# U also laid out transposed, longer DRAM runs, six accumulators and another dealing of gathered rows in a hybrid decoder block

## The chip, the cores and the metric

One core of a Trainium2 chip. The metric is the device time of one execution in microseconds. A run's time is that of the whole program; its profiled execution gives the trace.

## What is computed

One decoder block on x of 1024 tokens x 1024 channels, float32. Two mixers run on the normed input: stick-breaking attention (8 heads of 128) and a gated delta rule (8 heads, chunks); both are projected back, weighted by sigmoid gates and summed into x through w_out. Then a PEER feed-forward follows. Each token makes 8 queries, each of two halves, and takes the best 16 of 128 keys for either half, so the best 16 of the pairs: 128 experts of 16384 per token. With them

```
u   = u_tab[expert]                       # rows of 1024
act = gelu(einsum('td,ted->te', h, u))
out = einsum('te,ted->td', gate * act, v_tab[expert])
```

The tables u and v are 16384 x 1024 each, 64 MB.

## The kernel before

The tokens go in two halves of 512 (`half`, L1061): projections with stick-breaking attention (`sb_attend`), delta rule (`gdn_head`), gate logits, `merge`, `out_proj`, `ffn_norm`, `route`. Products of float32 are made as three matmuls of split operands (`mm3`, L68): `split` (L58) copies a value to a rounded `hi` on ACT and subtracts it to `lo` on DVE.

**Weights.** `load_w` (L87) loads a block of 256 columns of a weight in two DMAs of 512 KB on SP's queue; a run in DRAM is 256 floats, 1 KB. `keys_T` (L649) transposes the keys once at the start and keeps them in DRAM.

**The feed-forward goes two ways.** Four blocks of 128 tokens (0, 1, 4, 5) fetch each expert row that they need: `gather_rows` (L993) is a generator of 1024 steps. Each step gathers 128 rows of 4 KB, one per token, with an indirect DMA on POOL (L1016) into one of four row buffers (six in the dense loop), and uses them with one DVE instruction: L1019 (dot product, first 128 steps of a block) or L1021 (weighted sum, the other 128). Below, such a step is called a row. Rows are dealt to the other work: each call of `gather(phase)` (L1045) adds PACE[phase] (L30) to what is due, and as many rows are issued with the lowest priority, each ordered on DVE behind the last DVE instruction so far. The scheduler may place them later, not earlier. Only the second half has rows: 64 calls in attention, 80 in the delta rule, 16 each in logits, merge and out, 64 in the gate table, and 128 in the dense loop.

**The other four blocks (2, 3, 6, 7; 512 tokens) are computed densely against all 16384 experts.** `gate_table` (L808) makes, block by block, a table of gate weights: for 32 tokens at a time PE multiplies one-hot matrices (L851), ACT evicts into `gt_stg` (two buffers, L852) and SP writes 2 MB to `g_d` in DRAM (L854), 16 writes in all. A run of the write is 16 KB, a run of the read (L906) 32 floats x 4, 512 bytes. The dense loop (L965 to L986) then takes 128 chunks of 128 experts:

- `prep` (L870): load 128 rows of U, 512 KB; 8 transposes on PE (L877) into the bank pair `pz0`; split each half from PSUM (ACT and DVE).
- `scores` (L882): 24 matmuls of 512 columns (L891, L893) into `pmm`, gelu on ACT (L895). It prepares the next chunk's U.
- `weigh` (L915): multiply by the gate table (L922), split (L926, L913).
- `values` (L931): load 512 KB of V in runs of 2 KB, and split.
- 24 value matmuls per chunk (L71 to L73 through `mm3`) into four accumulators, two banks `pc` and two `pz1`, evicted after 8 chunks by DVE (L974). Then the next group begins, for the other 512 columns or the next 8 chunks.

Seven chunks of scores are asked for (PRE) while the gate table is made, between the blocks; the scheduler can run two more ahead, since `pmm` has two banks.

Of the kernel before, what the change touches and what calls it, by code (L numbers as in the profile page):

```python
# [7 lines left out]
F32 = mybir.dt.float32  # L8
F32R = mybir.dt.float32r
# [9 lines left out]
P = 128  # L19
D = 1024  # L20
# [4 lines left out]
GT = 32  # L25
KD = D // P
# [3 lines left out]
PACE = dict(sb=2.2, gdn=1.5, logits=2.5, merge=2.5, out=0.5, route=0, table=0.1, dense=5.25)  # L30
# [4 lines left out]
C_GS, C_GG = 7184, 8208  # L35


class Block:
# [48 lines left out]
    def load_w(self, src, c0, n=CB):  # L87

        hi = self.wp.tile([P, KD, n], F32R, name="w_hi")
        lo = self.wp.tile([P, KD, n], F32R, name="w_lo")  # L90
        for k0 in range(0, KD, 4):
            raw = self.wraw.tile([P, 4, n], F32, name="w_raw")
            self.nc.sync.dma_start(raw, src[k0 * P:(k0 + 4) * P, c0:c0 + n].rearrange("(k p) n -> p k n", p=P))
            for k in range(k0, k0 + 4, 2):
                self.split(hi[:, k:k + 2], lo[:, k:k + 2], raw[:, k - k0:k - k0 + 2])
        return hi, lo
# [131 lines left out]
    def sb_qk(self, hx, pair, col):  # L228

        nc, pool = self.nc, self.pj  # L230
        w = self.load_w(self.i["w_in"][0], col + pair * CB)
# [30 lines left out]
    def sb_v(self, hx, pair, v):  # L262
        w = self.load_w(self.i["w_in"][0], C_V + pair * CB)
# [110 lines left out]
    def gdn_gates(self, half, hx, pool):  # L374
# [3 lines left out]
        w = self.load_w(self.i["w_in"][0], C_BA, 16)  # L378
# [35 lines left out]
    def gdn_proj(self, half, hx, pair):  # L414
# [3 lines left out]
        for n, col in enumerate((C_GQ, C_GK, C_GV, C_GZ)):  # L418
            w = self.load_w(self.i["w_in"][0], col + pair * CB)
# [158 lines left out]
    def gate_logits(self, half, hx):  # L578
        nc = self.nc
        for br, gcol in enumerate((C_GS, C_GG)):  # L580
            for c in range(D // CB):
                w = self.load_w(self.i["w_in"][0], gcol + c * CB)
# [8 lines left out]
    def merge(self, half, mg, x2, pool):  # L591
        nc = self.nc
        part = pool.tile([P, KD, TH], F32, name="part")
        for br, (osrc, wname) in enumerate(((self.o_sb, "w_branch_sb"), (self.o_gdn, "w_branch_gdn"))):
# [8 lines left out]
            for c in range(D // CB):  # L603
                wb = self.load_w(self.i[wname][0], c * CB)
# [21 lines left out]
    def out_proj(self, half, mg, x2):  # L626

        nc = self.nc
        for c in range(2):
            w = self.load_w(self.i["w_out"][0], c * CB)  # L630
# [7 lines left out]
        ws = [self.load_w(self.i["w_out"][0], c * CB) for c in (2, 3)]  # L638
# [9 lines left out]

    def keys_T(self, kp):  # L649

        nc = self.nc
        kt = kp.tile([P, H, 2, P], F32, name="kt")
        for t, nm in enumerate(("peer_keys1", "peer_keys2")):
            raw = kp.tile([P, H, P], F32, name="kraw", bufs=2)
            nc.sync.dma_start(raw, self.i[nm][0].rearrange("h n d -> n h d"))
            for h0 in range(0, H, 4):
                ps = self.pzt([P, 4, P])
                for h in range(4):
                    nc.tensor.transpose(ps[:, h], raw[:, h0 + h], self.ident)
                nc.scalar.copy(kt[:, h0:h0 + 4, t], ps)  # L660
        nc.sync.dma_start(self.keys_d, kt)
# [510 lines left out]
```

## Time and profile before

| | us |
|---|---|
| median of 3 runs | 3900.24 |
| lowest, highest | 3888.91, 3903.44 |
| profiled execution | 3908.46 |
| its span | 3906.7 |
| mean granted clock of TensorE, as a share of full speed | 0.971 |

The span runs from the first to the last instruction; 1.8 us of the execution lie around it. TensorE shows 94% of the span, DVE 79%, ACT 45%, POOL 33%. Matmuls are pipelined, so what a matmul costs is read from start to start and not from its length. The chain that ended last lies on PE for 28% of the span, and the dense loop's score matmuls are its largest part.

### The profile page before, as it was taken

To read this page: it belongs to the slowest core of one execution; us is meant where nothing else is said; L and a number is where in the kernel's file an instruction comes from. 1 tells how busy PE (TensorE), PEld (TensorE's weight loads), DVE (VectorE), ACT (ScalarE), POOL (GpSimd) and SP (SyncE) were. 2 spreads that over 40 slices of the span, in tenths; PEclk is the share of its full clock that TensorE was granted. 3 is DMA by queue.
4 is the path that set the end of the run, shared out by engine and by line. 5 is a ranking of instruction groups with operands and counts; after the bars stand their busy time and mean duration, and the time that the engine had idled before them with its cause. 6 is when DMAs were issued, how large, how long until landed. Compare 5 with 4: busy or idle time off the path is not lost. (4 is left out here: it accounts for less than half of the span.)

```text
span 3906.7 us, 55712 instructions
## 1 busy us (share of the span) xinstructions
PE 3674.3 (94%) x19976; PEld 3077.4 (79%) x19976; DVE 3089.5 (79%) x6330; ACT 1753.0 (45%) x3986; POOL 1298.8 (33%) x1034
## 2 busy tenths in 40 slices
PE   8999999999999999998877995899999999999997
PEld 7878888787777688886666884788888888888886
DVE  4345554349988988888789998899898899899898
ACT  6755555333777655543322994222222222222321
POOL 0000000000144322233341113655566555566555
PEclk9999999999999999999888998999999999999998
DMA  5221114552387766578884568899999999999998
GB/s 141 86 83 50 55 49 127 167 190 88 103 275 263 240 196 190 161 229 290 309 283 147 214 230 305 307 353 363 334 362 355 332 354 352 335 360 351 351 347 297
DMA packets 448230, 939.72 MB, mean 241 GB/s; under 512 B 44113, under 2 KB 239697, under 8 KB 445521
## 3 DMA queue, kind: packets, MB, share of 16 engines
q0 software_dynamic: 147456, 536.94, 39.1%
q1 hardware_dynamic: 300496, 399.22, 30.5%
q8 instruction: 157, 2.57, 0.3%
q14 instruction: 121, 0.98, 0.1%
HBM read 865.27 MB, written 70.25 MB: 239 GB/s over the span
## 5 line engine op out<-in xcount | busy, mean ns | idle before, releaser
L1016 POOL DMA_INDIRECT gb_row<-peer_u,expert x512 | 670.0, 1309 | 1879.1 <-DVE expert L796 1013.5
L1016 POOL DMA_INDIRECT gb_row<-peer_v,expert x512 | 627.6, 1226 | 714.9 <-DVE gb_h L1021 464.1
L1021 DVE SCALAR_TENSOR_TENSOR gb_h<-gb_row,gb_act,gb_h 128x1024 f32<-128x1024 f32 x512 | 656.1, 1281 | 60.6 <-DMA gb_row<-peer_v,expert 33.1
L1019 DVE SCALAR_TENSOR_TENSOR gb_row<-gb_row,gb_h 128x1024 f32<-128x1024 f32 x512 | 613.0, 1219 | 97.4 <-DMA gb_row<-peer_u,expert 77.6
L891 PE MATMUL mm<-hf,ut 128*128 128x512 f32 x2048 | 514.2, 398 | 0.0
L891 PEld LDWEIGHTS mm<-hf,ut 128*128 128x128 f32 x2048 | 376.1, 188 | 70.7
L63 DVE TENSOR_TENSOR w_lo<-w_raw,w_hi 128x512 fp32r<-128x512 f32 (+1 forms) x456 | 298.4, 676 | 166.7 <-ACT w_hi L62 128.5
L62 ACT CAST w_hi<-w_raw 128x512 fp32r<-128x512 f32 (+1 forms) x456 | 262.9, 615 | 275.6 <-PE mm L72 127.5
L71 PE MATMUL mm<-h,w_hi 128*128 128x512 f32 (+1 forms) x784 | 322.4, 411 | 4.0 <-ACT pj L587 4.0
L73 PE MATMUL mm<-h,w_lo 128*128 128x512 f32 (+1 forms) x784 | 319.9, 408 | 0.0
L72 PE MATMUL mm<-h,w_hi 128*128 128x512 f32 (+1 forms) x784 | 319.2, 407 | 0.0
L71 PE MATMUL mm<-w_hi,h 128*128 128x256 f32 x1024 | 301.3, 295 | 9.2 <-DVE x L636 4.7
L73 PE MATMUL mm<-w_hi,h 128*128 128x256 f32 x1024 | 294.6, 289 | 5.7 <-DVE h L63 5.7
L926 ACT CAST d_a<-u_act 128x512 fp32r<-128x512 f32 x128 | 79.4, 621 | 484.7 <-DVE u_act L922 483.9
L72 PE MATMUL mm<-w_lo,h 128*128 128x256 f32 x1024 | 296.0, 289 | 0.7 <-DVE w_lo L63 0.7
L893 PE MATMUL mm<-hf,ut 128*128 128x512 f32 x1024 | 260.3, 391 | 0.0
L895 ACT ACTIVATE u_act<-mm 128x512 f32<-128x512 f32 x128 | 77.0, 601 | 390.2 <-PE mm L893 376.5
L71 PE MATMUL pz<-d_v,d_a 128*128 128x512 f32 x512 | 201.6, 394 | 45.1 <-ACT d_a L926 30.8
L62 ACT CAST d_v<-v_raw 128x1024 fp32r<-128x1024 f32 x128 | 134.3, 1050 | 208.0 <-PE pc L73 175.9
L893 PEld LDWEIGHTS mm<-hf,ut 128*128 128x128 f32 x1024 | 192.3, 188 | 38.9
L71 PEld LDWEIGHTS mm<-w_hi,h 128*128 128x128 f32 x1024 | 200.6, 196 | 17.3 <-DVE x L636 5.2
L73 PEld LDWEIGHTS mm<-w_hi,h 128*128 128x128 f32 x1024 | 200.7, 196 | 7.8 <-DVE h L63 5.9
(332 smaller groups left out, 8632.4 us busy)
## 6 DMA issues: line engine op xcount, KB each, us to landing
w_raw<-w_in SPq DMA_DIRECT2D x144, 512.0 KB
u_raw<-peer_u SPq DMA_DIRECT2D x128, 512.0 KB
v_raw<-peer_v SPq DMA_DIRECT2D x128, 512.0 KB
g_d<-gt_stg SPq DMA_DIRECT2D x16, 2048.0 KB
d_g<-g_d SPq DMA_DIRECT2D x31, 1024.0 KB
w_raw<-peer_w_q SPq DMA_DIRECT2D x32, 512.0 KB
gl<-pj SPq DMA_DIRECT2D x32, 256.0 KB
th<-gl SPq DMA_DIRECT2D x32, 256.0 KB
```

The lines of the kernel that those rows point to most:

```text
L62: nc.scalar.copy(hi, src)
L63: nc.vector.tensor_tensor(lo, src, hi.bitcast(F32), op=OP.subtract)
L71: mm(out, l[0], r[0], start=first, stop=False)
L72: mm(out, l[0], r[1], start=False, stop=False)
L73: mm(out, l[1], r[0], start=False, stop=last)
L891: mm(ps, ut[0][:, k], hx[a][:, k, x0:], start=k + a == 0, stop=False)
L893: mm(ps, ut[1][:, k], hx[0][:, k, x0:], start=False, stop=k == KD - 1)
L895: nc.scalar.activation(act, ps, AF.Gelu)
L926: nc.scalar.copy(hi, act)
L1016: nc.gpsimd.indirect_dma_start(out=r, out_offset=None, in_=self.i["peer_u" if p < n else "peer_v"][0], in_offset=bass.IndirectOffsetOnAxis ...
L1019: i = nc.vector.scalar_tensor_tensor(r, r, 1.0, h2, op0=OP.mult, op1=OP.mult, accum_out=act[:, q:q + 1])
L1021: i = nc.vector.scalar_tensor_tensor(acc, r, act[:, q:q + 1], acc, op0=OP.mult, op1=OP.add)
```

## The change

The inputs are laid out anew before the launch: weights in blocks of 256 columns so that a partition's run is 4 KB; keys already transposed; U a second time, transposed within each chunk (`u_t`); V so that a run is 4 KB (`v_t`). The gathers still read U and V as they were. `keys_T` goes, and `prep` loads U transposed and splits it from SBUF, without transposes. The gate table in DRAM is turned so that the writes have runs of 512 bytes and the reads in the loop runs of 8 KB (2 KB for the first, which comes in four parts). The loop's accumulators rotate over six banks (`pz0`, `pz1`, `pc`). Between the blocks of the gate table one chunk of scores is placed, three in all, and the other four behind the last matmul of the gate table. The dealing of rows changes in three places.

```
-PACE = dict(sb=2.2, gdn=1.5, logits=2.5, merge=2.5, out=0.5, route=0, table=0.1, dense=5.25)
+PACE = dict(sb=2.5, gdn=2.0, logits=2.5, merge=2.5, out=0.5, route=0, table=0.1, dense=4.8)
...
 def load_w
-            self.nc.sync.dma_start(raw, src[k0 * P:(k0 + 4) * P, c0:c0 + n].rearrange("(k p) n -> p k n", p=P))
+            self.nc.sync.dma_start(raw, src[c0 // CB][:, k0:k0 + 4])
...
 def gate_table
-                        mm(pg[:, u - u0], o2[:, u], o1[:, u], start=True, stop=True)
+                        self.last_gate = mm(pg[:, u - u0], o2[:, u], o1[:, u], start=True, stop=True)
...
-            nc.sync.dma_start(self.g_d[(n * P + c * GT) // GT], stg)
+            nc.sync.dma_start(self.g_d[:, :, (n * P + c * GT) // GT].rearrange("g p q t -> p g (q t)"),
+                              stg.rearrange("p (g q) t -> p g (q t)", q=GQ))
 def dense
+            ur = pool(name="ur", bufs=2)
             def prep(e1):
-                raw = up.tile([P, D], F32, name="u_raw")
-                nc.sync.dma_start(raw, U[e1 * P:(e1 + 1) * P, :])
+                raw = ur.tile([P, KD, P], F32, name="u_raw")
+                nc.sync.dma_start(raw, U[e1])
                 ut = [up.tile([P, KD, P], F32R, name=f"ut{a}") for a in range(2)]
-                for k0 in range(0, KD, 4):
-                    ps = self.pz.tile([P, 4, P], F32, name="pz0")
-                    for k in range(4):
-                        nc.tensor.transpose(ps[:, k], raw[:, (k0 + k) * P:(k0 + k + 1) * P], self.ident)
-                    self.split(ut[0][:, k0:k0 + 4], ut[1][:, k0:k0 + 4], ps)
+                self.split(ut[0], ut[1], raw)
                 return ut
...
+            def bank():
+                self.turn = (self.turn + 1) % 3
+                return (self.pc if self.turn == 2 else self.pz).tile([P, 512], F32, name=("pz0", "pz1", "pc")[self.turn])
...
-                nc.sync.dma_start(raw, V[e1 * P:(e1 + 2) * P, dh * 512:dh * 512 + 512].rearrange("(q p) d -> p q d", p=P))
+                nc.sync.dma_start(raw, V[e1 // 2, dh])
...
                     self.gate_table(n, blk, gt)
-                    for e1 in range(PRE * n // nb, PRE * (n + 1) // nb):
+                    if n < nb - 1:
+                        scores()
+                with self.tc.issue_after(self.last_gate.ins):
+                    while len(acts) < PRE:
                         scores()
...
-                    ps = [self.pc.tile([P, 512], F32, name="pc") if n % 2 else self.pz.tile([P, 512], F32, name="pz1")
-                          for n in range(nb)]
+                    ps = [bank() for n in range(nb)]
...
-        b.g_d = dr.tile([len(b.dense_blks) * P // GT, P, P, GT], F32, name="g_d")
+        b.g_d = dr.tile([P // GQ, P, len(b.dense_blks) * P // GT, GQ, GT], F32, name="g_d")
...
+    a["u_t"] = x["peer_u"][0].reshape(P, P, KD, P).transpose(0, 3, 2, 1)
+    a["v_t"] = x["peer_v"][0].reshape(P // 2, 2, P, 2, D // 2).transpose(0, 3, 2, 1, 4)
```

`issue_after` orders on PE alone: the instructions of its block that run on PE stand behind the last gate matmul.

## Rows read from the trace of the kernel before

**Rows 1.** The profile's page: busy time of each engine, and three of the lines that cut the span into 40 slices of 97.7 us (PE: busy share in tenths; DMA: busy share of the DMA engines in tenths; GB/s: what they moved).

```profile
PE 3674.3 (94%) x19976; PEld 3077.4 (79%) x19976; DVE 3089.5 (79%) x6330; ACT 1753.0 (45%) x3986; POOL 1298.8 (33%) x1034
...
PE   8999999999999999998877995899999999999997
...
DMA  5221114552387766578884568899999999999998
GB/s 141 86 83 50 55 49 127 167 190 88 103 275 263 240 196 190 161 229 290 309 283 147 214 230 305 307 353 363 334 362 355 332 354 352 335 360 351 351 347 297
```

**Rows 2.** The windows view, stretch by stretch: length, busy time (and instructions) of PE, weight loads, DVE, ACT and POOL, then granted clock, DMA share and GB/s. 970 to 1325 is the attention of the second half, 1325 to 1775 its delta rule, 1775 to 2125 merge, output projection, norm and routing, 2125 to 2372 the gate table, and the dense loop begins at 2403.

```profile
970.00:1325.00 355.00, 324.94 (x1801) 251.21 (x1801) 315.92 (x782) 273.35 (x737) 122.97 (x106) 0.95 0.64 210
1325.00:1775.00 450.00, 432.13 (x2687) 370.56 (x2686) 374.15 (x819) 234.46 (x594) 142.36 (x127) 0.98 0.65 206
1775.00:2125.00 350.00, 297.48 (x1451) 245.12 (x1449) 294.13 (x861) 108.76 (x193) 109.51 (x93) 0.92 0.77 262
2125.00:2372.00 247.00, 221.22 (x1470) 196.41 (x1470) 243.03 (x594) 211.97 (x490) 37.31 (x23) 0.94 0.59 216
2372.00:2403.00 31.00, 0.21 (x2) 0.10 (x1) 25.69 (x40) 3.25 (x5) 15.99 (x13) 0.54 1.00 345
...
2603.00:3697.00 1094.00, 1092.51 (x5187) 910.22 (x5186) 982.10 (x1307) 302.74 (x470) 648.17 (x490) 1.00 0.97 349
```

**Rows 3.** Groups of instructions by line on PE, from 2403 us to the end (L891 and L893: scores, 16 and 8 to a chunk; L71 to L73: here the value matmuls; L877: transposes of U, 8 to a chunk): busy, mean ns, idle time before them and what ended it.

```profile
L891 PE MATMUL mm<-hf,ut 128*128 128x512 f32 x1904 | 462.9, 395 | 0.0
...
L71 PE MATMUL pz<-d_v,d_a 128*128 128x512 f32 x512 | 201.6, 394 | 45.1 <-ACT d_a L926 30.8 <-DVE d_acc L974 14.2
...
L71 PE MATMUL pc<-d_v,d_a 128*128 128x512 f32 x512 | 200.7, 392 | 4.5 <-DVE d_acc L974 4.5
...
L877 PE MATMUL pz<-ident,u_raw 128*128 128x128 f32 x928 | 120.5, 272 | 0.9 <-DVE ut L63 0.8
```

**Rows 4.** PE's timeline in the dense loop: start, length, line, operation.

```profile
2446.00 3.79 PE L891 MATMUL mm<-hf,ut 128*128 128x512 f32 x16
...
2451.44 0.39 PE L71 MATMUL pz<-d_v,d_a 128*128 128x512 f32 x1
...
2456.89 1.03 PE L877 MATMUL pz<-ident,u_raw 128*128 128x128 f32 x8
2457.68 3.91 PE L891 MATMUL mm<-hf,ut 128*128 128x512 f32 x16
...
2463.24 0.39 PE L71 MATMUL pz<-d_v,d_a 128*128 128x512 f32 x1
```

**Rows 5.** The timeline of all engines where the gate table ends and the dense loop begins (brackets: idle before, and what ended it).

```profile
2358.24 2.91 ACT L842 ACTIVATE gt_o<-pz,gt_tr 128x128 f32<-128x128 f32 x8
...
2365.43 2.91 ACT L842 ACTIVATE gt_o<-pz,gt_tr 128x128 f32<-128x128 f32 x8
...
2370.06 2.05 PE L851 MATMUL pc<-gt_o,gt_o 128*128 128x128 f32 x16 [0.94 <-ACT gt_o L845]
...
2383.33 3.16 SPq L906 DMA_DIRECT2D d_g<-g_d  x5
...
2402.90 0.80 PE L71 MATMUL pz<-d_v,d_a 128*128 128x512 f32 x1 [30.79 <-ACT d_a L926]
```

**Rows 6.** Groups of instructions by line on DVE in the steady loop, 2603 to 3697 us.

```profile
L1019 DVE SCALAR_TENSOR_TENSOR gb_row<-gb_row,gb_h 128x1024 f32<-128x1024 f32 x256 | 303.5, 1219 | 29.8 <-DMA gb_h<-h2d 14.6 <-DMA gb_row<-peer_u,expert 14.5
L1021 DVE SCALAR_TENSOR_TENSOR gb_h<-gb_row,gb_act,gb_h 128x1024 f32<-128x1024 f32 x235 | 301.2, 1282 | 13.2 <-DMA gb_h<-x2d 7.6 <-DMA gb_row<-peer_v,expert 1.3
L63 DVE TENSOR_TENSOR ut<-pz,ut 128x512 fp32r<-128x512 f32 x186 | 119.3, 683 | 1.6 <-ACT ut L62 1.6
L63 DVE TENSOR_TENSOR d_v<-v_raw,d_v 128x1024 fp32r<-128x1024 f32 x94 | 116.0, 1234 | 2.0 <-ACT d_v L62 1.8
```

**Rows 7.** DMA queues from 2375 to 2382.3 us, when the last piece of the gate table is written (q1 is SP's queue): packets, MB, share of 16 engines' time.

```profile
q1 hardware_dynamic: 142, 2.10, 71.7%
```

**Rows 8.** The same from 2384.5 to 2400.3 us, when the first piece of the gate table is read back (q0 carries the gathers).

```profile
q0 software_dynamic: 889, 3.23, 56.9%
q1 hardware_dynamic: 4173, 2.10, 47.1%
```

**Rows 9.** Instructions that write or read the gate table in DRAM (minimum, median and maximum ns of the issue, first and last start).

```profile
L854 SPq DMA_DIRECT2D g_d<-gt_stg x16: 319/325/333, 2165.0 to 2372.8; - x16
```

**Rows 10.** Who waited for whom, over the whole span: us in total, times, longest.

```profile
POOL gb_row L1016 <- DVE gb_row L1019: 603.7, 190, 41.6
...
POOL gb_row L1016 <- DVE gb_h L1021: 481.3, 184, 21.7
...
ACT w_hi L62 <- DMA w_raw<-peer_w_q: 36.3, 13, 5.4
...
ACT w_hi L62 <- DMA w_raw<-w_in: 32.0, 13, 8.1
...
DVE gb_h L1021 <- DMA gb_h<-x2d: 19.5, 3, 11.9
```

**Rows 11.** Groups by line, whole span: the line of projection matmuls that waited longest for a split weight.

```profile
L73 PE MATMUL mm<-hf,w_lo 128*128 128x512 f32 x256 | 102.0, 398 | 2.4 <-DVE w_lo L63 2.3
```

**Rows 12.** DMA queues from 2603 to 3697 us.

```profile
q0 software_dynamic: 70251, 255.81, 63.3%
q1 hardware_dynamic: 86981, 124.68, 33.0%
```

## What the change was predicted to do

> **What bounds the kernel now.** The profiled execution took 3908.5 us, 8.3 us over the median of the three runs (3900.24); the sum below is made against it, and the difference is taken off at the end. A measurement of this kernel tells about 0.5% (19.5 us) from no change.
>
> I read the page's totals and slices first [rows 1]: TensorE is at 94%, and in the last third both TensorE and the DMA engines stand at 9 tenths or more. So I cut the span into stages [rows 2]. In the steady part of the dense loop (2603 to 3697 us) PE is busy 1092.5 of 1094 us at a granted clock of 1.00 (2.4 GHz), DMA has a share of 0.97 and DVE is busy 90%. The 93 preparations of U in that window [rows 6] (186 splits of half a U) make 11.76 us a step. The timeline shows what a step holds [rows 4]: 24 score matmuls take 5.44 us where no transposes precede them (2446.00 to 2451.44) and 6.35 us with them (2456.89 to 2463.24); the 24 value matmuls take 5.45 us (2451.44 to 2456.89). Nothing waits, so the loop is TensorE's own work, and a step without transposes is 10.86 us: 0.91 us less.
>
> Ahead of the loop TensorE has one hole: after the last gate matmul it stands 30.8 us until the first value matmul [rows 5]. In it SP sends the last piece of the gate table, waits for it, and loads it back.
>
> **The change, part by part.** *U transposed.* The 116 preparations after 2403 us (928 transposes by 8 [rows 3]) lose 0.91 us each: **-106 us**, if nothing else takes over. The other 12, in the table stage, are counted there. The split of U becomes one cast on ACT and one subtraction on DVE of 1024 columns. The V split has that form at 1.234 us against 2 x 0.683 for U now [rows 6]: DVE gets 0.13 us a step back, and ACT (303 of 1094 us busy [rows 2]) has room.
>
> *Scores moved.* Nine scores run before the hole (128 less the 119 behind it, 1904 matmuls by 16 [rows 3]); the new loop places three there and queues four behind the last gate matmul. Six more must run later, 6 x 5.44 = 33 us, and four of them, 21.8 us, lie in the hole. The hole itself changes: the write now has 512-byte runs. The written 2.10 MB took 71.7% of 7.3 us = 5.2 us of the sixteen DMA engines [rows 7]; the same bytes read in 512-byte runs took 47.1% of 15.8 us = 7.4 us [rows 8], the nearest price for the new write. The read-back gets runs of 2 KB in four parts and 15.8 us elapsed beside gathers should about halve. I take a chain of 25 us, 3 us of hole left, and a net of **+5 us**; ends: -2 (six scores fit) and +15 (a slow write).
>
> *Table stage.* PE loses 33 us of scores and 11 us of transposes there, ACT some 9 us of casts. But in the last chunks, which have no scores at all, the gated activations still start 7.19 us apart (2358.24, 2365.43 [rows 5]), 14.4 us a chunk, against 13.85 us a chunk over all sixteen (2165.0 to 2372.8 [rows 9]). The pace is the exchange between PE and ACT, not the scores. Ends -44 and +9; I take **-8 us**, ACT's share.
>
> *Six accumulators.* A group of four banks waits for its eviction; the waits of the first value matmul for it sum to 14.2 + 4.5 us [rows 3]. Two spare banks hide a normal eviction, but not one behind a DVE that itself waits 11.9 us at a time for the next block's row (DVE gb_h waits for x2d 19.5 us in all [rows 10]). Ends -19 and 0; **-5 us**.
>
> *Longer runs of the weights, keys ready made.* ACT waits 36.3 + 32.0 us for the two kinds of w_raw that it waits for most [rows 10]. Made of a quarter of the packets, a load should land sooner beside the gathers. But PE waits for the split weights 2.3 us on the line that waits longest [rows 11], so most of this is hidden: **-8 us**, with the 16 transposes of the keys in it; ends 0 and -34, half the wait.
>
> *Rows dealt out.* Due before the loop are now 64 x 2.2 + 80 x 1.5 + 16 x 5 + 16 x 0.5 + 64 x 0.1 = 355 rows; after the change 64 x 2.5 + 80 x 2.0 + 94.4 = 414, and the loop deals 4.8 a step. But a due row is not a done row. POOL's counts [rows 2] are gathers issued: 106 by 1325 us where 141 were due, 233 by 1775 where 261 and more were. POOL waits 604 and 481 us for DVE to finish with rows that it holds [rows 10]: they are loaded and stand in DVE's order, behind everything else. There is always a backlog, and a larger debt finds no new gaps. So I expect the dealing not to do what it says: about 349 rows issued at 2372 us as now (355 due), 65 more owed at the loop's entry, and 675 rows for the loop, not 610.
>
> What that costs is read from the queues in the loop [rows 12]. Gathers: 63.3% of 1094 us for 255.8 MB, that is 369 GB/s, or 1.42 us of the sixteen engines a row of 0.524 MB. SP's queue: 33.0%, or 3.88 us a step for 1.34 MB, at 345 GB/s; in runs of 4 KB and more I price it as the gathers, 3.63 us. A step at 4.8 rows asks 4.8 x 1.42 + 3.63 = 10.45 of 10.86 us, 96%, as now (5.27 x 1.42 + 3.88 = 11.36 of 11.76). With the backlog the whole asks 675 x 1.42 + 128 x 3.63 = 1423 us, where PE's side is 1534.7 (2372 to the end) - 106 + 5 - 5 = 1429. DMA at a share of 1.00, as it had in the hole [rows 2], would cost nothing; at the 0.965 of the loop it would be 1475, +46. DVE has 10.56 us a step now (982.1 / 93), and 9.85 at 4.8 rows, so it is pressed only while the backlog lasts. I take a share near 0.985, 1447 us: **+18 us**.
>
> Sum: -106 + 5 - 8 - 5 - 8 + 18 = -104, so 3804.5 by the profiled execution and **3796 us** by the median.
>
> **The rivals.** *The DMA engines become the bound.* For: the share of 0.97 and two engines at the same height. Against: that rate was asked for by TensorE's pace, and slices reach 363 GB/s [rows 1]. The loop's bytes are 675 x 0.524 + 128 x 1.34 = 525 MB; if no more than the 349 GB/s of the steady loop [rows 2] can be had, 1505 us, 58 more than I count: 3854. Below 343 GB/s the whole gain would be gone.
> The Trainium skill, "DMA: Bandwidth & Descriptors", section "Where 436 GB/s comes from", names about 358 GB/s as what HBM gives one core: by that limit the loop would take 525 / 0.358 = 1468 us and the kernel 3817. The slices at 362 and 363 GB/s are a little above that figure, so the trace does not bear it out as a hard limit.
>
> *The dealing does what it says.* Then the loop carries 610 rows and the +18 goes, while 65 rows of 1.28 us [rows 6] come into the attention and delta-rule stages. Their DVE is busy 316 of 355 and 374 of 450 us [rows 2]: 83 us of work into 115 us of idle time, at a cost between 0 and 83; with 30, 3808 us. Against: the backlog.
>
> *Slower: the gate table's writes hold up the table stage.* The write becomes 4096 runs of 512 bytes that share the engines with the gathers. Two staging buffers allow 13.85 us a write; above that ACT's copies wait on all but the first two. The read in such runs lasted 15.8 us beside eight gathers [rows 8]; that would cost 14 x 2 = 27 us, and twice that time 14 x 17.7 = 248 us: 4044. It outweighs the gain, with the 0.5%, from (104 + 19.5) / 14 + 13.85 = 22.7 us a write. Against: few gathers run in that stage (23 in 247 us [rows 2]), so the engines are free for the write, and its own work is about 7.4 us.
>
> **How the numbers follow.** Forecast 0.64; DMA bound 0.20, of which 0.04 below 343 GB/s; dealing works 0.08; slow writes 0.05; the remaining 0.03 goes half to no change. That gives faster 0.89, same 0.06, slower 0.05. The range: below, with the row term at 0, evictions at -15, the table stage at -25 and weights at -20, 3745; above, the DMA rival at 349 GB/s, 3858.
>
> **What would show it.** Right: no transposes behind U; 48 matmuls a step and steps of 10.9 us for much of the loop; scores directly behind the last gate matmul and a hole under 10 us; POOL's count at the loop's entry still near 350; DMA share 0.98 or more in the loop's first half, with more than 4.8 rows a step there. Wrong: steps of 11.3 us or more with TensorE waiting for ut or d_v, or DVE waiting for rows (DMA is the bound); over 400 gathers before the loop and longer attention and delta-rule stages; in the table stage ACT's copies waiting for the write to DRAM and chunks above 14 us.

## The result, and the profile after

The changed kernel takes **3933.31 us** (median of 4 runs, 3928.59 to 3940.64) against 3898.45 us before on the same chip: 1.010 times the time, 95% interval 1.0078 to 1.0123. It is slower by 1%, where 3796 us were forecast. The profiled execution took 3940.64 us. One execution of V loaded once, below, took 4443 us at a granted clock of 0.746 and is left out of its median. The lines of the code moved: scores are L885 and L887 now, the value matmuls L72 to L74, their evictions L974, the split L64, the gathered rows still L1016 (gather), L1019 and L1021 (DVE).

The windows view of the kernel after; columns as in [rows 2]:

```profile
970.00:1325.00 355.00, 322.54 (x1783) 249.64 (x1781) 309.24 (x748) 269.32 (x725) 119.24 (x104) 0.95 0.63 207
1325.00:1775.00 450.00, 430.02 (x2679) 368.27 (x2679) 372.53 (x821) 231.84 (x589) 147.93 (x125) 0.98 0.64 205
1775.00:2125.00 350.00, 297.56 (x1446) 245.30 (x1447) 296.25 (x846) 111.01 (x199) 114.78 (x96) 0.92 0.78 266
2125.00:2387.00 262.00, 202.30 (x1257) 168.29 (x1256) 248.79 (x612) 206.99 (x471) 36.33 (x24) 0.96 0.66 192
2387.00:2424.00 37.00, 23.18 (x93) 18.07 (x92) 20.41 (x29) 9.85 (x12) 12.82 (x11) 0.89 0.94 319
2424.00:2600.00 176.00, 142.35 (x584) 115.34 (x584) 117.17 (x152) 41.95 (x55) 72.56 (x53) 0.88 0.76 268
2603.00:3697.00 1094.00, 1029.93 (x4406) 843.07 (x4405) 981.60 (x1220) 287.48 (x372) 703.14 (x504) 0.97 0.95 355
```

Three things are to be seen against [rows 2]. POOL issued 104 + 125 + 96 + 24 = 349 gathers up to 2387 us, as before: the new dealing moved no row. From 2424 to 2600 us there is a jam: PE 142 of 176 us, the DMA engines at 0.76. And in the steady loop PE is no longer full (1030 of 1094 us, 1092.5 before).

What PE waits for in the loop, from the groups by line on PE from 2403 us to the end (these answer to [rows 3]; the transposes are gone):

```profile
L885 PE MATMUL mm<-hf,ut 128*128 128x512 f32 x1952 | 462.3, 389 | 0.0
L72 PE MATMUL pz<-d_v,d_a 128*128 128x512 f32 x680 | 276.5, 407 | 68.2 <-DVE d_acc L974 64.0 <-ACT d_a L919 4.3
...
L72 PE MATMUL pc<-d_v,d_a 128*128 128x512 f32 x344 | 140.0, 407 | 33.8 <-DVE d_acc L974 33.8
```

The first value matmul of a group waits 97.8 us in all for DVE's evictions, where it was 14.2 + 4.5 us. One of these waits, on PE's timeline, and then the same time on DVE's:

```profile
2862.93 3.79 PE L885 MATMUL mm<-hf,ut 128*128 128x512 f32 x16
2866.56 1.98 PE L887 MATMUL mm<-hf,ut 128*128 128x512 f32 x8
...
2869.51 0.39 PE L74 MATMUL pc<-d_v,d_a 128*128 128x512 f32 x1
2876.71 0.80 PE L72 MATMUL pz<-d_v,d_a 128*128 128x512 f32 x1 [6.81 <-DVE d_acc L974]
2877.30 0.63 PE L73 MATMUL pz<-d_v,d_a 128*128 128x512 f32 x1
2877.73 0.63 PE L74 MATMUL pz<-d_v,d_a 128*128 128x512 f32 x1
...
2882.41 3.79 PE L885 MATMUL mm<-hf,ut 128*128 128x512 f32 x16
...
2904.17 3.79 PE L885 MATMUL mm<-hf,ut 128*128 128x512 f32 x16
```

```profile
2866.48 1.23 DVE L1019 SCALAR_TENSOR_TENSOR gb_row<-gb_row,gb_h 128x1024 f32<-128x1024 f32 x1 [3.73 <-DMA gb_row<-peer_u,expert]
...
2868.77 1.22 DVE L1019 SCALAR_TENSOR_TENSOR gb_row<-gb_row,gb_h 128x1024 f32<-128x1024 f32 x1
...
2874.82 1.22 DVE L1019 SCALAR_TENSOR_TENSOR gb_row<-gb_row,gb_h 128x1024 f32<-128x1024 f32 x1
...
2875.97 1.28 DVE L974 TENSOR_TENSOR d_acc<-pz,d_acc 128x512 f32<-128x512 f32 x2
```

DVE stands 3.73 us for a row that has not landed, works through five rows and four other instructions, and only then comes to the evictions; PE has been waiting 6.81 us. Where nothing is waited for, two steps take 2904.17 - 2882.41 = 21.76 us, 10.88 each. PE's part of the change is there; DVE doesn't let it be used.

A wait costs more than its idle time. Behind this one PE's value matmuls start 0.43 us apart up to 2879.86 us, where they start 0.23 us apart ahead of it: the windows view gives a granted clock of 0.50 (1.2 GHz) from 2876.7 to 2879.8 us and of 1.00 from 2858 to 2869. In the steady loop 109 matmuls start so far apart; at 0.20 us each that is, by estimate, 22 us beside the 64 us in which PE is idle.

### The profile page after: what moved, and what is told of

The parts are those of the page before. It is cut to its first block, busy times and chain, and to the rows that moved or that the text cites. A ratio compares the mean times of both kernels' runs of the same rounds, so it can differ in the third digit from the quotient of the medians.

```text
span 3938.9 us, 53574 instructions
## 1 busy us (share of the span) xinstructions
PE 3609.4 (92%) x18936; PEld 2992.4 (76%) x18936; DVE 3077.7 (78%) x6196; ACT 1739.5 (44%) x3846; POOL 1354.1 (34%) x1034
## 5 line engine op out<-in xcount | busy, mean ns | idle before, releaser
L1016 POOL DMA_INDIRECT gb_row<-peer_u,expert x512 | 684.9, 1338 | 1896.9 <-DVE expert L793 1010.4
L1016 POOL DMA_INDIRECT gb_row<-peer_v,expert x512 | 668.1, 1305 | 674.9 <-DVE gb_h L1021 428.7
L1019 DVE SCALAR_TENSOR_TENSOR gb_row<-gb_row,gb_h 128x1024 f32<-128x1024 f32 x512 | 614.3, 1218 | 199.2 <-DMA gb_row<-peer_u,expert 179.4
L1021 DVE SCALAR_TENSOR_TENSOR gb_h<-gb_row,gb_act,gb_h 128x1024 f32<-128x1024 f32 x512 | 657.7, 1285 | 82.3 <-DMA gb_row<-peer_v,expert 63.9
L885 PE MATMUL mm<-hf,ut 128*128 128x512 f32 x2048 | 490.4, 391 | 6.6 <-DMA hf<-hd 6.6
L885 PEld LDWEIGHTS mm<-hf,ut 128*128 128x128 f32 x2048 | 385.7, 188 | 87.2 <-ACT ut L63 5.8
L64 DVE TENSOR_TENSOR w_lo<-w_raw,w_hi 128x512 fp32r<-128x512 f32 (+1 forms) x450 | 297.5, 682 | 166.4 <-ACT w_hi L63 129.4
L72 PE MATMUL pz<-d_v,d_a 128*128 128x512 f32 x680 | 276.5, 407 | 68.2 <-DVE d_acc L974 64.0
L72 PE MATMUL mm<-h,w_hi 128*128 128x512 f32 (+1 forms) x784 | 322.1, 411 | 3.3 <-ACT pj L598 3.3
L74 PE MATMUL mm<-h,w_lo 128*128 128x512 f32 (+1 forms) x784 | 319.9, 408 | 0.0
L73 PE MATMUL mm<-h,w_hi 128*128 128x512 f32 (+1 forms) x784 | 319.1, 407 | 0.0
L72 PE MATMUL mm<-w_hi,h 128*128 128x256 f32 x1024 | 300.2, 294 | 8.9 <-DVE x L647 4.9
L74 PE MATMUL mm<-w_hi,h 128*128 128x256 f32 x1024 | 294.2, 288 | 5.4 <-DVE h L64 5.4
L73 PE MATMUL mm<-w_lo,h 128*128 128x256 f32 x1024 | 295.3, 289 | 0.6 <-DVE w_lo L64 0.5
L74 PE MATMUL pz<-d_v,d_a 128*128 128x512 f32 x680 | 273.2, 402 | 0.8 <-DVE d_a L906 0.8
L73 PE MATMUL pz<-d_v,d_a 128*128 128x512 f32 x680 | 273.2, 402 | 0.0
L887 PE MATMUL mm<-hf,ut 128*128 128x512 f32 x1024 | 258.4, 393 | 9.6 <-DVE ut L64 9.6
L887 PEld LDWEIGHTS mm<-hf,ut 128*128 128x128 f32 x1024 | 193.7, 189 | 50.2 <-DVE ut L64 10.4
L72 PEld LDWEIGHTS mm<-w_hi,h 128*128 128x128 f32 x1024 | 199.8, 195 | 16.9 <-DVE x L647 5.7
L72 PEld LDWEIGHTS pz<-d_v,d_a 128*128 128x128 f32 x680 | 133.3, 196 | 104.2 <-DVE d_acc L974 70.7
```

Source lines behind the costliest of these rows:

```text
L64: nc.vector.tensor_tensor(lo, src, hi.bitcast(F32), op=OP.subtract)
L72: mm(out, l[0], r[0], start=first, stop=False)
L73: mm(out, l[0], r[1], start=False, stop=False)
L74: mm(out, l[1], r[0], start=False, stop=last)
L885: mm(ps, ut[0][:, k], hx[a][:, k, x0:], start=k + a == 0, stop=False)
L887: mm(ps, ut[1][:, k], hx[0][:, k, x0:], start=False, stop=k == KD - 1)
```

## The experiments

Times are medians against the kernel before on the same chip. "Hole" runs from the last gate matmul to the first value matmul, "loop" from the first to the last value matmul, "tail" from there to the end, each read from the starts in one profiled execution. PE's own floor for the loop is 128 x 10.88 us less seven scores already done (7 x 5.44): 1355 us.

| kernel | us | last gate matmul | hole | loop | tail |
|---|---|---|---|---|---|
| before | 3898 | 2371.8 | 31.1 | 1479.1 | 24.7 |
| changed | 3933 | 2385.7 | 38.0 | 1495.5 | 19.7 |
| old dealing | 3875 | 2382.5 | 31.9 | 1433.0 | 26.1 |
| four banks | 3929 | 2379.7 | 38.1 | 1489.3 | 18.6 |
| U alone | 3859 | 2371.9 | 25.0 | 1435.8 | 23.7 |
| scores between | 3921 | 2381.0 | 31.2 | 1482.3 | 18.4 |
| dealt, 3,000 | 3881 | 2426.3 | 75.2 | 1359.4 | 19.5 |
| V loaded once | 3876 | 2383.4 | 30.5 | 1428.4 | 25.0 |
| half the row work | 3787 | 2379.8 | 21.9 | 1362.5 | 20.5 |
| debt only | 3933 | 2383.0 | 36.5 | 1511.1 | 6.6 |
| dealt, 1,000 | 3986 | 2575.0 | 21.9 | 1368.0 | 19.5 |
| dealt, 1,000, scores between | 3978 | 2574.3 | 19.2 | 1360.3 | 18.5 |
| old dealing, scores between | 3866 | 2375.7 | 27.8 | 1438.5 | 24.9 |
| four row buffers | 4107 | 2389.7 | 33.0 | 1653.3 | 33.6 |
| owed rows on six | 3900 | 2372.9 | 32.2 | 1462.2 | 18.1 |
| multiplication on POOL | 3997 | 2364.5 | 29.2 | 1567.9 | 25.3 |
| eight row buffers | 3825 | 2374.8 | 31.9 | 1391.7 | 22.3 |
| U alone, eight buffers | 3832 | 2375.6 | 24.2 | 1410.8 | 22.1 |

### Which part of the change costs the time

My theory after the comparison (A): the rows owed at the loop's entry cost it. Rivals: the six banks (B), the place of the scores (C).

**The old dealing.**

```diff
-PACE = dict(sb=2.5, gdn=2.0, ..., dense=4.8)
+PACE = dict(sb=2.2, gdn=1.5, ..., dense=5.25)
```

> The changed kernel with the old dealing of rows (2.2 per attention, 1.5 per delta-rule step, 5.25 per dense chunk), all else changed. Theory A (some 60 rows owed at the loop's entry are carried through the loop as 5.5 rows a step, DVE and the DMA engines have no slack, and evictions stand behind rows in DVE's order): the debt goes, rows settle near 5.3 a step, the waits of the first value matmul at group switches (64.0 + 33.8 us) fall by half or more, about 3870 us. Theory B (the rotation over six banks makes those waits): unchanged waits, within 10 us of 3933. Theory C (the scores taken out of the table stage): also unchanged, near 3933.

3874.86 us, ratio 0.9943 (0.9922 to 0.9964): 58 us less than the changed kernel, nearly all in the loop. The first value matmuls of the groups wait 26.5 + 17.6 us for evictions, where it was 64.0 + 33.8. The jam is gone, as the windows view of this kernel shows:

```profile
2424.00:2600.00 176.00, 168.48 (x732) 138.43 (x731) 155.76 (x185) 50.85 (x64) 109.42 (x79) 0.98 0.96 361
2603.00:3697.00 1094.00, 1056.22 (x4579) 866.68 (x4578) 998.09 (x1237) 299.13 (x389) 707.99 (x504) 0.98 0.95 359
```

**Four banks again.**

```diff
-ps = [bank() for n in range(nb)]
+ps = [self.pc.tile(...) if n % 2 else self.pz.tile(..., name="pz1") for n in range(nb)]
```

> The changed kernel with the value accumulators on four banks in the old order, all else changed. Theory A: the waits at the group switches stay or grow, 3930 to 3960 us. Theory B (rotation over six banks costs): the waits fall to the 14 + 5 us of before, about 3855 us.

3928.92 us, ratio 1.0085 (1.0064 to 1.0106), which overlaps the changed kernel's. B falls; the six banks neither cost nor bring anything that can be measured.

**U alone, on the kernel before.**

```diff
-nc.sync.dma_start(raw, U[e1 * P:(e1 + 1) * P, :])
-... transposes ...
+nc.sync.dma_start(raw, U[e1])
+self.split(ut[0], ut[1], raw)
```

> The kernel before with one part of the change alone: U laid out transposed, no transposes on TensorE; scores, dealing, weights, gate table and accumulators as before. By my sum 116 x 0.91 us = 106 us less: about 3795 us with steps of 10.87 us if the old dealing leaves DVE and DMA enough room (Theory A). If the DMA engines or DVE bound the loop whatever the dealing, steps of 11.3 us and more and 3840 to 3880 us. Theory C says the scores between blocks keep the table stage and the hole as before (chunks of 13.85 us, hole 31 us).

3859.12 us, ratio 0.9901 (0.9883 to 0.9918). My sum for this part was -106; only 39 us come, and the loop gives 43. So even without a debt something else bounds the loop.

**The scores between the blocks again.**

```diff
-if n < nb - 1:
-    scores()
-... the rest behind the last gate matmul ...
+for e1 in range(PRE * n // nb, PRE * (n + 1) // nb):
+    scores()
```

> The changed kernel with the scores ahead of the loop placed as before (none, two, two and the rest after the blocks) and not held behind the last gate matmul. Theory C: the chunks go back to 13.9 us and the hole costs some 20 us less: about 3913 us. Theory A: the loop ends when its rows, DVE and DMA work end, so what is gained ahead of it is mostly given back: 3925 to 3935 us.

3921.41 us, ratio 1.0064 (1.0046 to 1.0082): 12 us less, C's smaller part. On the old dealing, below, the same edit is worth 9 us, and with 1,000 places 7. The intervals of each of these pairs overlap; what speaks for the gain is that all three have one sign.

**The debt without the new pace in the loop.**

```diff
-PACE = dict(sb=2.5, gdn=2.0, ..., dense=4.8)
+PACE = dict(sb=2.5, gdn=2.0, ..., dense=5.25)
```

> The changed kernel with 2.5 rows per attention and 2.0 per delta-rule step as in the change, but the old 5.25 per dense chunk: the debt at the loop's entry stays, the pace of 4.8 goes. Theory A: as the changed kernel, 3920 to 3945 us, with the jam at 2440 to 2545 us. Rival D (the pace of 4.8 does it): as with the old dealing, 3875 us.

3933.08 us, ratio 1.0092 (1.0075 to 1.0109): as the changed kernel. It is the debt, not 4.8.

### What bounds the loop once the debt is gone

Both run on the old dealing. The first leaves out 127 of 128 loads of V, the second half of the rows' arithmetic (shown for the dot product; the weighted sum is cut the same way).

```diff
-raw = up.tile(...)
-nc.sync.dma_start(raw, V[e1 // 2, dh])
+if k == 0:
+    self.v_raw = up.tile(...)
+    nc.sync.dma_start(self.v_raw, V[e1 // 2, dh])
+raw = self.v_raw
```

> The changed kernel with the old dealing, and V's table loaded from DRAM only once: every later split reads the same tile, so the values are not the reference's and 127 of 128 loads of 0.524 MB (67 MB of some 523 MB in the loop) are left out; the work of TensorE, ACT and DVE stays. If the rate of the DMA engines (358 GB/s over the loop of the kernel with the old dealing, 1433 us) sets the loop's time, 67 MB are worth 187 us and the loop falls until TensorE or DVE bounds it: 1370 to 1390 us, 3815 to 3830 us. If DVE's order of work sets it, less than 15 us: 3860 to 3875.

```diff
-i = nc.vector.scalar_tensor_tensor(r, r, 1.0, h2, ...)
+i = nc.vector.scalar_tensor_tensor(r[:, :512], r[:, :512], 1.0, h2[:, :512], ...)
```

> The changed kernel with the old dealing, and DVE's two instructions on a gathered row taken over half of its 1024 columns: half of the rows' arithmetic is left out, the gathers stay whole. If the DMA engines set the loop, it stays within 15 us of 1433 us, and the time falls only by what the stages ahead of the loop gain. If DVE (91% busy, 5.3 rows x 1.28 us of a step of 11.2 us) sets it, the loop falls to 1370 to 1390 us and the time to 3810 to 3830 us.

V loaded once: 3876.00 us, ratio 0.9951 (0.9934 to 0.9967), as the old dealing alone. Half the row work: 3787.34 us, ratio 0.9713 (0.9684 to 0.9741). The steady loop in the windows view, first with V loaded once, then with half the row work:

```profile
2603.00:3697.00 1094.00, 1057.39 (x4592) 868.03 (x4591) 996.80 (x1239) 300.81 (x388) 708.25 (x503) 0.99 0.87 314
```

```profile
2603.00:3697.00 1094.00, 1089.81 (x4797) 901.72 (x4796) 777.76 (x1284) 331.43 (x406) 622.13 (x526) 1.00 0.98 375
```

With 13% fewer bytes the loop stays (1428.4 against 1433.0 us) although the DMA share falls to 0.87: the rate of the DMA engines was not its bound. With half the row work on DVE it falls to 1362.5 us, PE is full again, and the DMA engines deliver 375 GB/s. **DVE bounds the loop, by its work and by what it waits for in order.** This run doesn't separate the two: a row that is used up sooner also gives its buffer back sooner. The runs with four and with eight row buffers below bear on that. The Trainium skill, "DMA: Bandwidth & Descriptors", section "Where 436 GB/s comes from", says that some 358 GB/s of HBM bind a core's transfers; a mean of 375 over 1094 us lies above it, so here, with one core running, the measurement decides against that limit. No run here shows what two cores get.

How DVE spends a step is seen in its groups by line with the old dealing, 2603 to 3697 us:

```profile
L1021 DVE SCALAR_TENSOR_TENSOR gb_h<-gb_row,gb_act,gb_h 128x1024 f32<-128x1024 f32 x248 | 319.3, 1287 | 27.0 <-DMA gb_row<-peer_v,expert 13.1 <-DMA gb_h<-x2d 9.8
L1019 DVE SCALAR_TENSOR_TENSOR gb_row<-gb_row,gb_h 128x1024 f32<-128x1024 f32 x256 | 304.4, 1220 | 48.3 <-DMA gb_row<-peer_u,expert 27.1 <-DMA gb_h<-h2d 20.3
L64 DVE TENSOR_TENSOR ut<-u_raw,ut 128x1024 fp32r<-128x1024 f32 x96 | 117.1, 1220 | 0.0
```

96 steps in 1094 us are 11.40 us each, of which DVE works 998.09 / 96 = 10.40 and waits (27.0 + 48.3) / 96 = 0.78 for rows and the blocks' vectors; some 0.2 more go to ACT's casts. It would have to do it all in PE's 10.88.

### Can the rows be moved ahead of the loop?

```diff
-with self.later(1000000):
+with self.later(3000):
```

> The changed kernel with one number changed: the rows are scheduled 3,000 places behind the instruction where they fall due, not 1,000,000. In the order of DVE's program 421 rows then stand ahead of the first eviction, against 370: the dealing does what it says. Theory A (the rows owed at the loop's entry cost the time): the debt, the stretch of 2424 to 2600 us with TensorE busy 142 of 176 us and most of the waits at the group switches go; the loop carries 610 rows; the loop from the first to the last value matmul falls from 1495 us to 1390 to 1420, the stages ahead grow by 0 to 83 us (51 rows of 1.28 us into DVE's idle time): 3830 to 3890 us. Rival D (the pace of 4.8 rows a step, not the debt, upsets the loop): near 3933 or above, since the stages ahead grow and the loop stays.

3881.26 us, ratio 0.9957 (0.9943 to 0.9971), 52 us less than the changed kernel. 420 gathers (not 359) are issued by the first value matmul and the loop falls by 136 us to PE's floor, but the first value matmul comes 77.7 us later: 1.3 us a row, all of it on the path. Of the 61 rows 40 went into the table stage and the hole (72 gathers from the first gate matmul to the first value matmul, 32 in the changed kernel), where DVE had little room; the other 21 went ahead of it. With 1,000 places they go further ahead:

```diff
-with self.later(1000000):
+with self.later(1000):
```

> The changed kernel with one number changed: the rows are scheduled 1,000 places behind the instruction where they fall due. In DVE's order 408 rows then stand ahead of the first gate table instruction (323 in the changed kernel, 344 with 3,000 places), so the dealing takes place in the attention, delta-rule and merge stages and not in the table stage. Theory A with DVE as the loop's bound: about 610 rows are left for the loop, TensorE's 10.88 us a step bounds it: 1355 to 1370 us between the first and the last value matmul as with 3,000 places (1359), the hole back to 30 to 40 us (it was 75), the stages ahead longer by 20 to 60 us: 3815 to 3860 us. Against: each row pulled ahead costs its 1.28 us on the path of those stages, 85 rows or 109 us: 3880 to 3910 us.

3985.63 us, ratio 1.0229 (1.0208 to 1.0251). The loop is at its floor (1368.0), but the first value matmul comes 173.2 us later for 61 rows, 2.8 us each, more than twice what a row costs DVE. My expectation missed, even its worse branch. The waits of this kernel from 970 to 2125 us show where a row costs more than its own time:

```profile
ACT w_hi L63 <- DMA w_raw<-w_in: 132.4, 27, 20.1
...
DVE gb_row L1019 <- DMA gb_row<-peer_u,expert: 73.9, 55, 5.3
PEld mm L74 <- DVE w_lo L64: 46.0, 8, 13.1
```

In the changed kernel the same three are 25.9, 63.1 and 3.2 us. So what grew is the wait for weights: they arrive and are split late, and PE then waits for them; DVE itself stands hardly longer for gathers. How the earlier rows delay the weights is not shown. DVE's idle time ahead of the loop (115 us in the prediction's count) could not take the rows for nothing.

> The same, with the scores ahead of the loop placed between the blocks of the gate table as before. If the scores' place costs the changed kernel some 12 to 16 us ahead of the loop, 12 to 16 us below the run without it, since TensorE and no longer DVE bounds the loop: 3800 to 3845 us. If the row debt alone decides, the same as without it within 6 us.

(the same, with the edit of the scores shown above) 3978.21 us, ratio 1.0212 (1.0194 to 1.0231); 7 us less, against 12 to 16 expected, and far above the 3800 to 3845 us.

### Why owed rows cost more than others

A row's buffer is chosen where the row falls due: of four ahead of the loop, of six in it. Four buffers for all rows, on the old dealing:

```diff
-self.row_bufs += [(gp2, f"gb_row{4 + k}") for k in range(2)]
```

> The changed kernel with the old dealing and four row buffers in the loop instead of six. Theory A says that owed rows are slow because they were laid on the four buffers that exist ahead of the loop: then the whole loop runs at the rate of the stretch from 2460 to 2545 us of the changed kernel, with DVE waiting for each row; the loop grows from 1433 to 1550 us or more and the time to 3990 us or more. If the number of buffers doesn't matter (the DMA engines' rate or DVE's work sets the rows' rate): within 15 us of 3875 us.

4106.67 us, ratio 1.0534 (1.0514 to 1.0554). Its steady loop, in the windows view and in DVE's groups by line:

```profile
2603.00:3697.00 1094.00, 947.41 (x3935) 769.66 (x3934) 864.32 (x1061) 254.81 (x331) 612.35 (x431) 0.92 0.87 309
...
L1020 DVE SCALAR_TENSOR_TENSOR gb_h<-gb_row,gb_act,gb_h 128x1024 f32<-128x1024 f32 x216 | 277.2, 1283 | 100.8 <-DMA gb_row<-peer_v,expert 90.6 <-DMA gb_h<-x2d 6.9
L1018 DVE SCALAR_TENSOR_TENSOR gb_row<-gb_row,gb_h 128x1024 f32<-128x1024 f32 x216 | 259.6, 1223 | 113.0 <-DMA gb_row<-peer_u,expert 94.8 <-DMA gb_h<-h2d 16.8
```

DVE waits 90.6 + 94.8 us for rows, where it waited 13.1 + 27.1 with six buffers. 431 rows in 1094 us on four buffers are 10.15 us for one buffer's round. The DMA view of the kernel with the old dealing, over the whole span, ends its rows of issues with the median time in us from issue to landing:

```profile
gb_row<-peer_u,expert POOLq DMA_INDIRECT x512, 7.1
gb_row<-peer_v,expert POOLq DMA_INDIRECT x512, 7.2
```

That time runs from the start of POOL's gather, so POOL's own 1.4 us lies in it; in the steady loop of that kernel it is 7.8 us. With 1.25 us on DVE a round there is 9.05 us at the least, near the 10.15 measured here (this run has no landings): the round is nearly full, and on four buffers their number sets the rows' rate. Six buffers at 504 rows have 13.0 us for a round, so there, by this count, a buffer is short only where rows come in bunches; that is argued, not traced. Then the owed rows of the changed kernel were given six:

```diff
-while self.due >= 1:
+while self.due >= 1 and (phase == "dense" or self.dealt < 355):
+    self.dealt += 1
```

> The changed kernel with its new dealing, but what is due ahead of the loop beyond 355 rows is given its buffers only in the loop: the 59 owed rows come with the first dense chunk and rotate over six buffers, not four. If the owed rows are slow because they are confined to the four buffers that exist ahead of the loop: the jam after 2440 us shrinks and the time comes near the kernel with the old dealing, 3870 to 3890 us. If a debt is costly in any form, since all owed rows stand in DVE's order ahead of the evictions: 3920 to 3945 us.

3900.45 us (10 runs), ratio 1.0009 (0.9997 to 1.0022), between the two expectations: 33 of the 58 us of the debt go with its four buffers, 25 stay (in the loop 33 and 29 of 62). From 2424 to 2600 us PE is busy 159 us here, 142 in the changed kernel and 168 with the old dealing, so the jam shrinks and doesn't vanish. The edit also moves the owed rows in DVE's order, into the first dense chunk, so the buffers' part is not shown quite by itself.

### Relieving DVE without leaving work out

```diff
-nc.vector.tensor_tensor(a3, a3, gts[e1 // GQ][:, :, e1 % GQ], op=OP.mult)
+nc.gpsimd.tensor_tensor(a3, a3, gts[e1 // GQ][:, :, e1 % GQ], op=OP.mult)
```

> The kernel with U alone transposed, and the multiplication of the activations by the gate table (0.685 us a step) moved from DVE to POOL. If DVE's work bounds the loop, 0.685 of some 11.2 us a step goes from it: the loop falls from 1436 us towards TensorE's 1360, at most 76 us: 3785 to 3810 us, if POOL, with 65% of its time busy, takes it in without holding gathers up. If it does hold them up (POOL works in order, and the multiplication waits for ACT), DVE waits longer for rows: 3850 to 3920 us.

3996.55 us, ratio 1.0263 (1.0245 to 1.0282): worse, and for another reason than I wrote. DVE's groups by line in this kernel, 2603 to 3697 us:

```profile
L1015 DVE SCALAR_TENSOR_TENSOR gb_row<-gb_row,gb_h 128x1024 f32<-128x1024 f32 x255 | 310.7, 1253 | 33.4 <-DMA gb_row<-peer_u,expert 16.9 <-DMA gb_h<-h2d 16.2
...
L909 DVE TENSOR_TENSOR d_a<-u_act,d_a 128x512 fp32r<-128x512 f32 x87 | 59.9, 689 | 168.0 <-ACT d_a L922 159.6 <-issue 8.4
```

Rows are not held up (16.9 us of waiting, 33.6 with U alone). DVE stands 160 us for ACT's cast of the product (11.7 with U alone), with the rows behind it in order; ACT waits 790 us for POOL's product. On POOL the product stands in order behind gathers, which wait 112 + 94 us for DVE.

The old dealing and the old places of the scores together:

> The changed kernel with the old dealing and the old places of the scores; what is left of the change is U transposed, the longer runs, the ready keys and the six accumulators. If the scores' place is what stands between the old dealing (3875 us) and U alone (3859 us): 3857 to 3865 us. If the gate table's layout or the six accumulators are: 3870 to 3877 us.

3865.99 us, ratio 0.9915 (0.9896 to 0.9933): the interval overlaps that of U alone, so the longer runs, the ready keys and the six banks bring nothing that can be measured here, taken together. On this version, and on U alone, two more row buffers in the place of a third of V's split tiles:

```diff
-LEAD, SL, PRE, NA, AB, VB, GB = 6, 0, 7, 7, 10, 6, 2
+LEAD, SL, PRE, NA, AB, VB, GB = 6, 0, 7, 7, 10, 4, 2
-self.row_bufs += [(gp2, f"gb_row{4 + k}") for k in range(2)]
+self.row_bufs += [(gp2, f"gb_row{4 + k}") for k in range(4)]
```

> The changed kernel with the old dealing and the old places of the scores (3866 us), with eight row buffers in the loop instead of six; their space comes from the split tiles of V (four of each half in use instead of six, so V is split two products earlier instead of four). Four buffers instead of six made the loop 1653 us instead of 1433. If DVE's waits for gathered rows (some 40 us in the steady part of the loop) come from too few gathers in flight: they go, and the loop falls from 1438 us to 1390 to 1410: 3820 to 3840 us. If the DMA engines can't deliver rows faster than now (355 GB/s with the loads of the tables): 3860 to 3870 us. If V split later makes TensorE wait for d_v: above 3870 us, with that wait in the list.

> The same on the kernel with U alone transposed (3859 us; shorter runs in the tables' loads, four accumulators): 3815 to 3840 us if more gathers in flight are what the loop lacks; 3855 to 3865 us if the DMA engines' rate bounds them, and then more likely here than with the longer runs, since its DMA share is 0.97 to 1.00 where the other has 0.95.

**3824.63 us**, ratio 0.9825 (0.9803 to 0.9846), and 3831.71 us, ratio 0.9835 (0.9813 to 0.9858): the first beats both kernels, by 73 and 109 us, with all of the change in it but the dealing and the scores' place. Its steady loop:

```profile
2603.00:3697.00 1094.00, 1070.23 (x4663) 878.93 (x4662) 1023.11 (x1266) 306.31 (x395) 765.32 (x520) 0.99 0.97 370
```

Both times are as expected, though DVE's waits for rows only fall, from 27.3 + 23.2 us to under 30 in the steady loop. Against the same kernel with six buffers DVE works 93.5% instead of 90.9%, and 520 rows pass instead of 505. A step's work on DVE is as before, by estimate 10.5 us (1023.11 us over 4663 matmuls by 48, and 994.79 over 4519), but its idle time falls from 1.05 to 0.73 us a step, 41 of the 47 us that the loop loses: so the gain is that DVE stands less, not that it works less. The two versions' intervals overlap: the lengths of the loads' runs are not told apart here either. What of the last 37 us between this loop (1391.7) and PE's floor is DVE's work and what its waits was not tried, and neither was an eviction taken out of the rows' order.

## Why the prediction was wrong

The sum was -104 us against the profiled time of before; the profiled executions differ by +32.

**The step that failed is the rows' term: "DVE has 10.56 us a step now (982.1 / 93), and 9.85 at 4.8 rows, so it is pressed only while the backlog lasts", and with it +18 us priced by the DMA share alone.** The same paragraph had counted 675 rows for the loop, that is 5.27 a step: the backlog lasts to the end. At that count DVE's work is 10.56 - 0.13 = 10.43 us of a step of 10.88, 96%, for an engine that was at 90% in the loop [rows 2] and waits in order for gathers and casts. At those 90% a step would have been 10.43 / 0.898 = 11.6 us; with the old dealing it was 11.40. The runs show what stood in its place: from PE's loop (1362.5 with half the row work) to 1433.0 us, 71 us, by DVE's row work and waits (two more row buffers give back 47 us of this kind with all of DVE's work in place); from there to 1495.5, 62 us, by the debt. That is 133 us where 18 were counted, 115 of the 136 by which the forecast missed. The other terms missed by some 33 to 38 us together, and the loop at PE's pace is some 17 us shorter than the sum had it (1479.1 - 106 - 5 + 2 x 5.44 = 1379), so the parts account for the whole within 5 us.

**That the dealing moves no row** was right: 349 gathers by 2387 us, as forecast. I took the debt for 65 rows of ordinary price. That owed rows have only four buffers, and that they stand in DVE's order ahead of evictions, was in the code and not counted.

**U transposed, -106**: PE's side was right to 0.02 us (a step of 10.88 for 10.86 us), and four kernels whose loop PE bounds (1359 to 1368 us) show that it is there to be had. U alone gave 39, and 66 with eight row buffers; the rest went to DVE and its waits.

**Table stage, -8**: +10 in fact, just past my upper end of +9. The writes of the gate table are 14.5 us apart on the mean now; the row that answers to [rows 9]:

```profile
L851 SPq DMA_DIRECT2D g_d<-gt_stg x16: 359/366/388, 2168.7 to 2386.6; - x16
```

(2386.6 - 2168.7) / 15 = 14.53 against 13.85 us. That is near the 14.4 us of the last chunks without scores [rows 5]; I had them as the end and took ACT's share as the value.

**Scores moved, +5**: 7 to 12, within its ends. The hole is 38.0 us and not the chain of 25 that I took, although four scores run in it. First SP's list of waits (2125 to 2430 us; total, times, longest), then the timeline:

```profile
SPq L870 <- DVE ut L64: 25.3, 2, 16.7
...
2386.58 0.36 SPq L851 DMA_DIRECT2D g_d<-gt_stg  x1
...
2403.70 0.34 SPq L870 DMA_DIRECT2D u_raw<-u_t  x1
2403.73 2.11 PE L887 MATMUL mm<-hf,ut 128*128 128x512 f32 x8 [3.25 <-DVE ut L64]
...
2415.78 3.61 PE L887 MATMUL mm<-hf,ut 128*128 128x512 f32 x8 [6.32 <-DVE ut L64]
```

The load of U behind the last write waits 16.7 us for DVE's subtraction in the split of an earlier U. DVE comes to it at 2402.45 us, 6.3 us after ACT's cast, behind four gathered rows, for the first of which it stood 6.30 us; the read of the gate table stands behind the load in SP's order. So DVE's order of rows lengthens the hole too. The write in 512-byte runs has also become slower: in the kernel with the old dealing and the scores between, where no load of U stands between, SP waits 16.7 us for it, 10.2 before.

**Six accumulators, -5, and longer runs, -8**: neither can be seen (four banks the same; U alone the same as all of it).

**The rivals.** The DMA engines as the bound, whose price set the upper end of the range, is excluded by V loaded once. My sign for it, DVE waiting for rows, did appear (50.6 + 25.8 us in the steady loop) and would have misled: the DMA engines had room, the row buffers and DVE's order had none. By my own terms its limit was 338 GB/s (525 MB in 1447 + 104 us) and not 343, and the low end of the range 3739 and not 3745 us; neither bears on the outcome. "The dealing does what it says" was priced at 30 us for 65 rows; made true, it costs 77.7 or 173.2. The slow writes did not come in the table stage: no wait of ACT for the write stands in the list. None named DVE.

## What to carry to other kernels

Before a bound is lifted, work out the next engine's work per step at the count that the step will really have, and hold it against the share that this engine has ever reached in that stage, not against 100%. A queue of work in arrears is served by the buffers it was given when it fell due, and on an in-order engine it stands ahead of work that others wait for. Two runs, one without half of an engine's work and one without part of the bytes, tell which of the two bounds a stage where both stand above 90%; whether the engine's work or its standing in order costs the time takes a third, here the one with more buffers.

## What was not expected of the hardware

How much two row buffers are worth: four instead of six made the loop 220 us longer (1433.0 to 1653.3), eight instead of six 47 us shorter (1438.5 to 1391.7), with gathers of 0.524 MB that land in 7.8 us (median of the steady loop with the old dealing). The run with eight also gave up a third of V's split tiles. On POOL the multiplication of 128 x 512 took 1.38 us (0.685 on DVE), and beside it DVE's weighted sum of a row (L1017 there) took 1.363 us instead of 1.288 us with U alone. The Trainium skill, "SBUF — State Buffer", section "SBUF: two separate sides", says that DVE with two inputs from SBUF and POOL reading SBUF lock each other out; the longer instruction agrees in direction, and no run here separates that lock from other causes.
